# Second SwiGLU product: weight sums and their split as two steps a unit apart, a third raw buffer, operands loaded behind the weights

## Chip, cores, metric

The kernel runs on one core of a Trainium2 chip. The metric is device time in microseconds (us) of one execution.

## What is computed

One inference step of a decoder trunk of two layers, over 1,056 tokens: a prompt of 1,024 and 8 samples of 4. Layer 0 mixes tokens by windowed attention, layer 1 by a gated linear recurrence; behind each mixer stands a SwiGLU of width D_FF = 2,816 on the model width 1,024. All is float32. The part at stake is the second line of this function, `(...) @ w_out`, in both layers:

```python
def swiglu(h, w_in, w_out):
    g, u = jnp.split(h @ w_in, 2, axis=-1)
    return (jax.nn.silu(g) * u) @ w_out
...
xp = xp + swiglu(rms_norm(xp, ffn_norm[layer]), w_ffn_in[layer], w_ffn_out[layer])
xs = xs + swiglu(rms_norm(xs, ffn_norm[layer]), w_ffn_in[layer], w_ffn_out[layer])
```

## The kernel before

Activations lie transposed, model width on the partitions, in three tiles of tokens, 384, 384 and 288 wide. Each float32 product is made of three products of fp32r parts (`mm3`, L291): high by high, high by low, low by high. So every weight is split when it has been loaded into a raw tile: ACT copies it into the high part (L83), VectorE (DVE) subtracts that for the low part (L87). The raw tiles of 128x1024 rotate over two buffers (NRAW); the DMA that fills one (L81) is issued by SyncE (SP).

The second SwiGLU product takes 256 rows of D_FF plainly (`outs`: the operands `h`, read from `hd`), 144 matmuls, and the other 2,560 in five chunks of 512 (`mixed`, `unit`). A unit is a chunk c and a pair of output blocks mp, 20 in a layer. It multiplies 2x2 blocks (two token tiles by two halves of the chunk) in seven products instead of eight, each of 6 matmuls of 384 columns, and the third token tile plainly: two products of 12 matmuls of 288 columns. That makes 66 matmuls; DVE adds each of nine results to the residual stream x (L1001). The last chunk's units have 42, and its plain products come later, between steps of the norm that follows. The seven products use four blocks of the weight itself (`w`) and four sums of its blocks (`ws`). For these `MixSums.prep` runs four GpSimd (POOL) operations on the raw tile in place (L159 to L162), once L87 has read it; then `split` makes a high part on ACT (L329) and a low part on DVE (L330).

A unit's products go to PSUM banks A, B and Dk, eight banks in rotation; A takes three or four of them one after the other, so the next one on A can't begin before DVE's add has read the one ahead. The order of the products in a unit is A (`b11`), Dk (`t3`), B (`b21`), A (`t2`), the first plain one, Dk (`t4`), A (`t1`), the second plain one, A (`b22`).

The other operand of these products, sums of the activations of a chunk, is made earlier and written to DRAM (`od`; the high parts by L870, the low parts by L871). A chunk has nine operands (seven of 768 KB, two of 576 KB), loaded back by `Operand.prep` (L184) into places that are given out and freed: 6 slots of the pool `hp` (`hs`) and 12 of the pool `gp`, 18 in all, two chunks. Weights and sums take one of 6 slots (`wslots`).

TensorE (PE) and SP run in the order of the program (MAN); the order on DVE, ACT and POOL is a scheduler's. Where in the program the loads and splits stand is set by `drive`: it lists what the items need, in order of first use (`needs`, and `ahead` behind them), and behind each item it calls `prep` on the next of the list until one has no place. A unit's `ahead` in chunk c, at mp = 2 and 3, is the next chunk's operands; the first unit's `ahead` is also its own nine operands, and on SP these come in front of the last twelve writes to `od` and of the second weight.

Of the kernel before, what the change touches and what calls it, by code (L numbers as in the profile page):

```python
# [55 lines left out]
class Slots:  # L56
    def __init__(self, names):
        self.free = list(names)
# [8 lines left out]
class Weight:  # L67


    def __init__(self, src, ext=False):  # L70
        self.src, self.ext, self.t, self.slot, self.raw = src, ext, None, None, None

    def prep(self, k, early=False):
        nc = k.nc
        ok = [s for s in k.wslots.free if self.ext or s[0] is k.gw]
        if not ok:
            return False
        self.slot = ok[0]
        k.wslots.free.remove(self.slot)
        raw = self.raw = k.gw.tile([P, 1024], F32, name=k.nm("raw"), tag="raw", bufs=NRAW)  # L80
        nc.sync.dma_start(raw, self.src)  # L81
        self.t = self.slot[0].tile([P, 2, 1024], F32R, name=k.nm("w"), tag=self.slot[1])
        nc.scalar.activation(self.t[:, 0, :], raw, AF.Copy)  # L83
        if early:
            k.early.append((self.t, raw))
        else:
            nc.vector.tensor_tensor(self.t[:, 1, :], raw, self.t[:, 0, :].bitcast(F32), OP.subtract)  # L87
        return True
# [55 lines left out]

class MixSums:
# [5 lines left out]
    def prep(self, k):  # L151
        nc = k.nc
        if not k.wslots.free:
            return False
        self.slot = k.wslots.get()
        r = self.w.raw
        a, b, c, d = (r[:, i * 256:(i + 1) * 256] for i in range(4))
        tt = nc.gpsimd.tensor_tensor
        tt(d, c, d, OP.add)  # L159
        tt(c, a, c, OP.subtract)  # L160
        tt(a, d, a, OP.subtract)  # L161
        tt(b, b, a, OP.subtract)  # L162
        self.t = self.slot[0].tile([P, 2, 1024], F32R, name=k.nm("w"), tag=self.slot[1])
        k.split(self.t[:, 0, :], self.t[:, 1, :], r)
        return True
# [26 lines left out]
class Item:  # L192
    def __init__(self, fn, needs=(), frees=None, ahead=()):
        self.fn, self.needs, self.ahead = fn, list(needs), list(ahead)
# [38 lines left out]
class Kern:  # L233
# [33 lines left out]
    def drive(self, items):  # L267
        need = [w for it in items if isinstance(it, Item) for w in it.needs + it.ahead]
# [4 lines left out]
        for it in items:  # L273
# [4 lines left out]
            else:  # L278
# [5 lines left out]
                while todo and todo[0].prep(self):  # L284
                    todo.pop(0)
# [525 lines left out]
    def ffn_phase(self, l, before, after):  # L811
# [266 lines left out]

        def mixed():
# [5 lines left out]
            for c in range(NCH):  # L1085
                o, last = O[c], c == NCH - 1
                for mp in range(4):
                    w = Weight(I[f"wz{l}"][c, mp], True)
                    s = MixSums(w)
                    end = mp == 3  # L1090
                    nxt = [] if last else {2: O[c + 1][:5], 3: O[c + 1][5:]}.get(mp, [])
                    if last:
                        items.append(Item(lambda a, b, *x, mp=mp: unit(a, b, x, mp, True), [w, s] + o[:7],
                                          [s] + (o[:7] if end else [])))
                        rest.append(Item(lambda a, x, y, mp=mp: [plain(a, (x, y), m, True) for m in (2 * mp, 2 * mp + 1)]
                                         and None, [w] + o[7:], [w] + (o[7:] if end else [])))
                    else:
                        items.append(Item(lambda a, b, *x, mp=mp: unit(a, b, x[:7], mp, False, x[7:]), [w, s] + o,
                                          [w, s] + (o if end else []), nxt))
# [13 lines left out]
        m[0].ahead += m[0].needs[2:]  # L1113
# [380 lines left out]
```

## Time and profile before

| what | value |
|---|---|
| median of 3 runs | 2238.1 us (2237.57 to 2241.82) |
| the profiled execution | 2240.83 us |
| its span in the trace | 2239.0 us |
| mean granted TensorE clock | 0.984 |
| PE, DVE, ACT, POOL busy | 96%, 68%, 45%, 11% of the span |

The span goes from the first to the last instruction that the trace holds; the execution's time has the 1.8 us around it too. Engines are PE (matmul), PEld (weight load, beside PE), DVE, ACT, POOL and SP. In a row of instructions the tiles are written out<-in, with the buffers' numbers left out; a group has its count, busy time and mean ns, and behind the bar the idle time ahead of it and who ended it. The stretch of the second SwiGLU product in chunks is 882 to 1141 us in layer 0 and 1978.4 to 2220.2 us in layer 1.

### The profile page before, as it was taken

How to read it: one execution, taken by the hardware profiler on the slowest of the kernel's cores; microseconds unless marked ns; L12 is line 12 of the kernel's file. 1: busy time of each engine (PE TensorE's matmuls, PEld its weight loads, DVE VectorE, ACT ScalarE, POOL GpSimd, SP SyncE). 2: the span in 40 equal slices, each digit the busy share in tenths (PEclk: the TensorE clock that was granted, in tenths of full speed). 3: DMA queues.
4: the chain of work that ended last, by engine and by line, in shares of the span. 5: the costliest groups of instructions: out<-in, count | busy, mean ns of one | idle time of the engine just before them, and what ended most of it. 6: DMA issues, size and time to landing. Idle time of an engine off the chain costs nothing.

```text
span 2239.0 us, 35153 instructions
## 1 busy us (share of the span) xinstructions
PE 2145.5 (96%) x13608; PEld 2109.3 (94%) x13608; DVE 1514.5 (68%) x2976; ACT 1010.8 (45%) x1835; POOL 242.8 (11%) x328
## 2 busy tenths in 40 slices
PE   9999998999999999989899999999999999999987
PEld 8899988999999999978899989999999999998886
DVE  6877678856566666546685788788666666665556
ACT  5666665434444342111257887744444444411123
POOL 1223230000000001113200000000000000013222
PEclk9999999999999999989999999999999999999998
DMA  5322424133433438445112123431333333575432
GB/s 188 106 96 87 138 76 136 46 125 106 153 129 110 145 128 304 190 156 230 48 49 65 66 67 113 125 93 63 133 133 126 130 136 125 191 270 184 177 130 78
DMA packets 122607, 288.47 MB, mean 129 GB/s; under 512 B 13576, under 2 KB 77640, under 8 KB 122440
## 3 DMA queue, kind: packets, MB, share of 16 engines
q1 hardware_dynamic: 121680, 285.91, 37.1%
q8 instruction: 106, 1.74, 0.3%
q14 instruction: 61, 0.50, 0.1%
q10 hardware_dynamic: 760, 0.33, 0.1%
HBM read 212.34 MB, written 75.84 MB: 129 GB/s over the span
## 4 chain that ended last, share of the span: by engine, by line
PE 75%; DVE 11%; ACT 5%; POOL 5%; issue 2%; DMA 2%; SPq 0%; POOLq 0%; ACTq 0%; DVEq 0%
PE mm L291 71%; DVE w L87 3%; DVE x L1001 2%; ACT w L329 1%; DVE w L330 1%; POOL raw L160 1%; ACT w L83 1%; POOL raw L161 1%; POOL raw L159 1%; POOL raw L162 1%; PE pt L602 1%; PE s L554 1%; DMA raw<-in_wq 1%; DVE s L572 1%; ACT s L579 1%
## 5 line engine op out<-in xcount | busy, mean ns | idle before, releaser
L291 PE MATMUL mm<-xn,w 128*128 128x384 f32 (+1 forms) x5808 | 930.2, 318 | 13.7 <-DVE x L737 4.8
L291 PEld LDWEIGHTS mm<-xn,w 128*128 128x128 f32 x5808 | 904.4, 189 | 19.4 <-issue 5.0
L291 PE MATMUL mm<-o,w 128*128 128x384 f32 (+1 forms) x2640 | 447.4, 330 | 49.8 <-DVE x L1001 35.8
L291 PEld LDWEIGHTS mm<-o,w 128*128 128x128 f32 x2640 | 434.0, 193 | 61.9 <-DVE x L1001 44.5
L87 DVE TENSOR_TENSOR w<-raw,w 128x1024 fp32r<-128x1024 f32 x246 | 299.4, 1223 | 123.6 <-ACT w L83 121.8
L83 ACT ACTIVATE w<-raw 128x1024 fp32r<-128x1024 f32 x248 | 261.5, 1056 | 223.1 <-PE mm L291 128.4
L291 PE MATMUL mm<-T,w 128*128 128x384 f32 x1920 | 351.5, 338 | 0.9 <-ACT sg L969 0.8
L291 PEld LDWEIGHTS mm<-T,w 128*128 128x128 f32 x1920 | 338.8, 188 | 1.6 <-ACT sg L969 1.5
L1001 DVE TENSOR_TENSOR x<-mm,x 128x384 f32<-128x384 f32 (+1 forms) x416 | 211.9, 531 | 119.4 <-PE mm L291 118.4
L159 POOL TENSOR_TENSOR raw<-raw 128x256 f32<-128x256 f32 x40 | 30.6, 764 | 1264.9 <-DVE w L87 810.2
L329 ACT ACTIVATE w<-raw 128x1024 fp32r<-128x1024 f32 x40 | 42.4, 1060 | 259.1 <-POOL raw L162 259.1
L330 DVE TENSOR_TENSOR w<-raw,w 128x1024 fp32r<-128x1024 f32 x40 | 49.9, 1248 | 88.8 <-ACT w L329 88.8
L594 POOL TENSOR_SCALAR s<-s,sm 128x256 f32<-128x256 f32 (+1 forms) x128 | 84.3, 676 | 206.5 <-DVE sm L592 93.5
L291 PE MATMUL mm<-att,w 128*128 128x384 f32 (+1 forms) x576 | 97.3, 324 | 0.3 <-DVE att L330 0.3
L291 PEld LDWEIGHTS mm<-att,w 128*128 128x128 f32 x576 | 91.3, 188 | 2.5 <-DVE att L330 0.5
L291 PE MATMUL mm<-y,w 128*128 128x384 f32 (+1 forms) x576 | 93.5, 322 | 0.0
L291 PEld LDWEIGHTS mm<-y,w 128*128 128x128 f32 x576 | 92.4, 188 | 0.0
L579 ACT ACTIVATE s<-s,sm 128x256 f32<-128x256 f32 (+1 forms) x128 | 61.7, 484 | 47.1 <-DVE sm L576 47.0
L868 ACT ACTIVATE hi<-e 128x384 fp32r<-128x384 f32 x80 | 41.8, 523 | 84.2 <-DVE e L992 28.5
L346 ACT ACTIVATE sq<-x 128x384 f32<-128x384 f32 (+1 forms) x105 | 51.0, 491 | 59.4 <-DVE x L1001 38.8
L116 DVE TENSOR_TENSOR w<-raw,w 128x1024 fp32r<-128x1024 f32 x40 | 48.9, 1223 | 35.5 <-ACT w L114 35.4
L976 ACT ACTIVATE sg<-sg 128x384 f32<-128x384 f32 x40 | 21.0, 525 | 91.4 <-DVE sg L975 91.4
(210 smaller groups left out, 2381.7 us busy)
## 6 DMA issues: line engine op xcount, KB each, us to landing
o<-od SPq DMA_DIRECT2D x70, 768.0 KB, 8.5
od<-hi SPq DMA_DIRECT2D x140, 192.0 KB, 2.0
raw<-in_wg SPq DMA_DIRECT2D x44, 512.0 KB, 4.0
raw<-in_wu SPq DMA_DIRECT2D x44, 512.0 KB, 5.0
raw<-in_wz SPq DMA_DIRECT2D x40, 512.0 KB, 4.2
od<-e SPq DMA_DIRECT2D x80, 192.0 KB, 2.0
raw<-in_wq SPq DMA_DIRECT2D x24, 512.0 KB, 3.6
raw<-in_wo SPq DMA_DIRECT2D x24, 512.0 KB, 3.5
```

What stands on the lines that cost most here:

```text
L83: nc.scalar.activation(self.t[:, 0, :], raw, AF.Copy)
L87: nc.vector.tensor_tensor(self.t[:, 1, :], raw, self.t[:, 0, :].bitcast(F32), OP.subtract)
L116: tt(d[:, 1, :], g, d[:, 0, :].bitcast(F32), OP.subtract)
L159: tt(d, c, d, OP.add)
L291: mm = lambda *a, **k: self.nc.tensor.matmul(*a, skip_group_check=more, **k)
L329: nc.scalar.activation(hi, src, AF.Copy)
L330: nc.vector.tensor_tensor(lo, src, hi.bitcast(F32), OP.subtract)
L346: nc.scalar.activation(sq[:, :W], self.xview(t, kb), AF.Square)
L579: nc.scalar.activation(s[:, j, :N], s[:, j, :N], AF.Exp, bias=sm[:, 1, j:j + 1], accum_out=sm[:, 3, j:j + 1])
L594: nc.gpsimd.tensor_scalar(s[:, j, :N], s[:, j, :N], sm[:, 4, j:j + 1], 1.0, op0=OP.mult, op1=OP.mult)
L868: nc.scalar.activation(hi.bitcast(F32R), src, AF.Copy)
L1001: tt(x, ps[:, :WID[t]], x, OP.add)
```

## The change

- The four POOL steps become a step of their own (`Mix`), and `MixSums` only splits.
- Each item has a list `order` in place of `ahead`. Unit u's is: its weight and sums, the next unit's weight and sums, three of the next chunk's operands (from mp = 1 on), then the split of its own sums, then its operands. So the split of sums u comes behind the load, the split and the sums of weight u+1. 
- Every third weight has its raw tile not in the two rotating buffers but in a slot of `hp`, which it takes from the operands' places for good (`third`): 17 are left.
- `drive` no longer stops at an operand that has no place, but goes on to what stands behind it in the list. It still stops at a weight or sums without a place.
- The first chunk's operands are no longer ahead; they come behind the first two weights and the first split of sums.

Lines move by 1 in front of the change and by up to 18 behind it: L81 becomes L82, L83 L84, L87 L88, L184 L195, L329 and L330 L347 and L348, L870 and L871 L888 and L889, L1001 L1019; POOL's four are L156 to L159.

```diff
--- before.py
+++ after.py
@@ -67,17 +67,18 @@
 class Weight:
 
 
-    def __init__(self, src, ext=False):
-        self.src, self.ext, self.t, self.slot, self.raw = src, ext, None, None, None
+    def __init__(self, src, ext=False, place=None):
+        self.src, self.ext, self.place, self.t, self.slot, self.raw = src, ext, place, None, None, None
 
     def prep(self, k, early=False):
         nc = k.nc
         ok = [s for s in k.wslots.free if self.ext or s[0] is k.gw]
-        if not ok:
+        raw = ok and (self.place() if self.place else k.gw.tile([P, 1024], F32, name=k.nm("raw"), tag="raw", bufs=NRAW))
+        if not raw:
             return False
+        self.raw = raw
         self.slot = ok[0]
         k.wslots.free.remove(self.slot)
-        raw = self.raw = k.gw.tile([P, 1024], F32, name=k.nm("raw"), tag="raw", bufs=NRAW)
         nc.sync.dma_start(raw, self.src)
         self.t = self.slot[0].tile([P, 2, 1024], F32R, name=k.nm("w"), tag=self.slot[1])
         nc.scalar.activation(self.t[:, 0, :], raw, AF.Copy)
@@ -142,26 +143,36 @@
         self.slots.put(self.slot)
 
 
-class MixSums:
+class Mix:
 
 
     def __init__(self, w):
-        self.w, self.t, self.slot = w, None, None
+        self.w, self.t = w, None
 
     def prep(self, k):
-        nc = k.nc
-        if not k.wslots.free:
-            return False
-        self.slot = k.wslots.get()
         r = self.w.raw
         a, b, c, d = (r[:, i * 256:(i + 1) * 256] for i in range(4))
-        tt = nc.gpsimd.tensor_tensor
+        tt = k.nc.gpsimd.tensor_tensor
         tt(d, c, d, OP.add)
         tt(c, a, c, OP.subtract)
         tt(a, d, a, OP.subtract)
         tt(b, b, a, OP.subtract)
+        self.t = r
+        return True
+
+
+class MixSums:
+
+
+    def __init__(self, w):
+        self.w, self.t, self.slot = w, None, None
+
+    def prep(self, k):
+        if not k.wslots.free:
+            return False
+        self.slot = k.wslots.get()
         self.t = self.slot[0].tile([P, 2, 1024], F32R, name=k.nm("w"), tag=self.slot[1])
-        k.split(self.t[:, 0, :], self.t[:, 1, :], r)
+        k.split(self.t[:, 0, :], self.t[:, 1, :], self.w.raw)
         return True
 
     def free(self, k):
@@ -190,8 +201,9 @@
 
 
 class Item:
-    def __init__(self, fn, needs=(), frees=None, ahead=()):
-        self.fn, self.needs, self.ahead = fn, list(needs), list(ahead)
+    def __init__(self, fn, needs=(), frees=None, order=None):
+        self.fn, self.needs = fn, list(needs)
+        self.order = self.needs if order is None else list(order)
         self.frees = self.needs if frees is None else list(frees)
         self.halves = [self]
 
@@ -265,7 +277,7 @@
                 self.nc.gpsimd.tensor_tensor(w[:, 1, c], raw[:, c], w[:, 0, c].bitcast(F32), OP.subtract)
 
     def drive(self, items):
-        need = [w for it in items if isinstance(it, Item) for w in it.needs + it.ahead]
+        need = [w for it in items if isinstance(it, Item) for w in it.order]
         todo = self.todo = []
         for w in need:
             if w not in todo:
@@ -281,8 +293,14 @@
                 post = it.fn(*[w.t for w in it.needs])
                 for w in it.frees:
                     w.free(self)
-                while todo and todo[0].prep(self):
-                    todo.pop(0)
+                i = 0
+                while i < len(todo):
+                    if todo[i].prep(self):
+                        todo.pop(i)
+                    elif isinstance(todo[i], Operand):
+                        i += 1
+                    else:
+                        break
                 if post:
                     post()
 
@@ -1076,27 +1094,37 @@
             return [Item(lambda a, b, h, t=t: h_out(a, b, h, t), w + [h[t]],
                          (w if t == 2 else []) + [h[t]]) for t in range(NT)]
 
+        def third():
+
+            if "raw" not in T:
+                if not hs.free:
+                    return None
+                T["raw"] = hs.free.pop()
+            t = self.hp.tile([P, 4 * WMAX], F32, name=self.nm("raw"), tag=T["raw"])
+            return t[:, :1024]
+
         def mixed():
 
             pools = [(lambda: self.hp, hs), (lambda: self.gp, self.slots)]
             O = [[Operand(lambda c=c, i=i: OD[c, i], WMAX, pools) for i in KEEP] + [Operand(lambda c=c, i=i: OD[c, i], WID[2], pools) for i in range(2)]
                  for c in range(NCH)]
             items, rest = [], []
-            for c in range(NCH):
-                o, last = O[c], c == NCH - 1
-                for mp in range(4):
-                    w = Weight(I[f"wz{l}"][c, mp], True)
-                    s = MixSums(w)
-                    end = mp == 3
-                    nxt = [] if last else {2: O[c + 1][:5], 3: O[c + 1][5:]}.get(mp, [])
-                    if last:
-                        items.append(Item(lambda a, b, *x, mp=mp: unit(a, b, x, mp, True), [w, s] + o[:7],
-                                          [s] + (o[:7] if end else [])))
-                        rest.append(Item(lambda a, x, y, mp=mp: [plain(a, (x, y), m, True) for m in (2 * mp, 2 * mp + 1)]
-                                         and None, [w] + o[7:], [w] + (o[7:] if end else [])))
-                    else:
-                        items.append(Item(lambda a, b, *x, mp=mp: unit(a, b, x[:7], mp, False, x[7:]), [w, s] + o,
-                                          [w, s] + (o if end else []), nxt))
+            units = [(c, mp) for c in range(NCH) for mp in range(4)]
+            w = [Weight(I[f"wz{l}"][c, mp], True, third if (4 * c + mp) % 3 == 2 else None) for c, mp in units]
+            x = [Mix(y) for y in w]
+            s = [MixSums(y) for y in w]
+            for u, (c, mp) in enumerate(units):
+                o, last, end = O[c], c == NCH - 1, mp == 3
+                order = [w[u], x[u]] + ([w[u + 1], x[u + 1]] if u + 1 < len(units) else [])
+                order += (O[c + 1][3 * mp - 3:3 * mp] if mp and not last else []) + [s[u]] + o
+                if last:
+                    items.append(Item(lambda a, b, *y, mp=mp: unit(a, b, y, mp, True), [w[u], s[u]] + o[:7],
+                                      [s[u]] + (o[:7] if end else []), order))
+                    rest.append(Item(lambda a, y, z, mp=mp: [plain(a, (y, z), m, True) for m in (2 * mp, 2 * mp + 1)]
+                                     and None, [w[u]] + o[7:], [w[u]] + (o[7:] if end else [])))
+                else:
+                    items.append(Item(lambda a, b, *y, mp=mp: unit(a, b, y[:7], mp, False, y[7:]), [w[u], s[u]] + o,
+                                      [w[u], s[u]] + (o if end else []), order))
             return items, rest
 
         n0, n1 = after
@@ -1110,7 +1138,6 @@
             L += blocks(f)
         p = outs()
         m, q = mixed()
-        m[0].ahead += m[0].needs[2:]
         L += p
         for i, x in enumerate(m):
             if l == 0 and i < DB:
```


The order on PE and on POOL stays as it was. Three places elsewhere:

DVE in layer 1, start of the eighth unit, before. L87 makes the low part of the weight two units on, L330 that of its sums (both from raw_20759), and L1001 adds a bank (mm) to a tile of x:

```order
L87 TENSOR_TENSOR w_20761<-raw_20759,w_20761 128x1024
L1001 TENSOR_TENSOR x_1987<-mm_20771,x_1987 128x384
L1001 TENSOR_TENSOR x_3467<-mm_20773,x_3467 128x384
L1001 TENSOR_TENSOR x_1987<-mm_20772,x_1987 128x384
L330 TENSOR_TENSOR w_20768<-raw_20759,w_20768 128x1024
L1001 TENSOR_TENSOR x_1987<-mm_20771,x_1987 128x384
L1001 TENSOR_TENSOR x_4440<-mm_20802,x_4440 128x288
```

The same unit now; its nine adds are the rows L1019. L348 in the first row makes the low part of the next unit's sums, L88 that of the weight three units on, and L348 in the last row that of the sums two units on:

```order
L348 TENSOR_TENSOR w_20763<-raw_20578,w_20763 128x1024
L88 TENSOR_TENSOR w_20768<-raw_20766,w_20768 128x1024
L1019 TENSOR_TENSOR x_1987<-mm_20775,x_1987 128x384
L1019 TENSOR_TENSOR x_3467<-mm_20777,x_3467 128x384
L1019 TENSOR_TENSOR x_1987<-mm_20776,x_1987 128x384
L1019 TENSOR_TENSOR x_1987<-mm_20775,x_1987 128x384
L1019 TENSOR_TENSOR x_4440<-mm_20806,x_4440 128x288
L1019 TENSOR_TENSOR x_1987<-mm_20777,x_1987 128x384
L1019 TENSOR_TENSOR x_3467<-mm_20775,x_3467 128x384
L1019 TENSOR_TENSOR x_4440<-mm_20834,x_4440 128x288
L1019 TENSOR_TENSOR x_3467<-mm_20775,x_3467 128x384
L348 TENSOR_TENSOR w_20863<-raw_20674,w_20863 128x1024
```

Three adds stood between a weight's low part and its sums'. Now the unit's nine adds follow one another without a split between them, and the sums' split at its end reads raw_20674, whose weight was split before the unit.

DVE in layer 0, the fifth unit, before. L330 makes the low part of that unit's sums, L87 that of the next unit's weight:

```order
L1001 TENSOR_TENSOR x_1986<-mm_9994,x_1986 128x384
L330 TENSOR_TENSOR w_9791<-raw_9782,w_9791 128x1024
L1001 TENSOR_TENSOR x_3466<-mm_9996,x_3466 128x384
L1001 TENSOR_TENSOR x_1986<-mm_9995,x_1986 128x384
L1001 TENSOR_TENSOR x_1986<-mm_9994,x_1986 128x384
L87 TENSOR_TENSOR w_9878<-raw_9876,w_9878 128x1024
L1001 TENSOR_TENSOR x_4439<-mm_10025,x_4439 128x288
```

and now. The first L88 and L348, both from raw_9789, make the low parts of the next unit's weight and sums, the second L88 that of the weight after it:

```order
L1019 TENSOR_TENSOR x_1986<-mm_10002,x_1986 128x384
L1019 TENSOR_TENSOR x_3466<-mm_10004,x_3466 128x384
L88 TENSOR_TENSOR w_9791<-raw_9789,w_9791 128x1024
L1019 TENSOR_TENSOR x_1986<-mm_10003,x_1986 128x384
L1019 TENSOR_TENSOR x_1986<-mm_10002,x_1986 128x384
L348 TENSOR_TENSOR w_9982<-raw_9789,w_9982 128x1024
L88 TENSOR_TENSOR w_9885<-raw_9883,w_9885 128x1024
L1019 TENSOR_TENSOR x_4439<-mm_10033,x_4439 128x288
```

A unit's sums are now split in the unit ahead of it, and their low part stands two adds behind the weight's.

SP in layer 1, ahead of the first unit, before: the last three of the first chunk's nine operands (L184), then the first two of twelve writes to od (L870 for a high part, L871 for a low one). The first weight (in_wz) stands ahead of the nine, the second behind the twelve:

```order
L184 DMA o_19772<-od_15246 128x1536
L184 DMA o_19774<-od_15247 128x4x288
L184 DMA o_19776<-od_15248 128x4x288
L870 DMA od_15277<-hi_19787 128x384
L871 DMA od_15277<-e_2583_19640 128x384
```

and now: the last four of the twelve writes, then the first operands of the nine. The first two weights stand ahead of the twelve:

```order
L888 DMA od_15281<-hi_19795 128x384
L889 DMA od_15281<-e_2563_19453 128x384
L888 DMA od_15282<-hi_19800 128x384
L889 DMA od_15282<-t_19771 128x384
L195 DMA o_19858<-od_15240 128x1536
L195 DMA o_19860<-od_15241 128x1536
L195 DMA o_19862<-od_15242 128x1536
L195 DMA o_19864<-od_15243 128x1536
```

The nine operands have moved behind the twelve writes, the second weight in front of them.

More of the change, by code (lines that the diff above doesn't have):

```diff
@@ L142, in free @@
         self.slots.put(self.slot)
+class Mix:
+    def __init__(self, w):
+        self.w, self.t = w, None
+    def prep(self, k):
+        r = self.w.raw
+        a, b, c, d = (r[:, i * 256:(i + 1) * 256] for i in range(4))
+        tt = k.nc.gpsimd.tensor_tensor
+        tt(d, c, d, OP.add)
+        tt(c, a, c, OP.subtract)
+        tt(a, d, a, OP.subtract)
+        tt(b, b, a, OP.subtract)
+        self.t = r
+        return True
 class MixSums:
@@ L155, in prep @@
         self.slot = k.wslots.get()
-        r = self.w.raw
-        a, b, c, d = (r[:, i * 256:(i + 1) * 256] for i in range(4))
-        tt = nc.gpsimd.tensor_tensor
[L159 to L162, printed above, removed]
         self.t = self.slot[0].tile([P, 2, 1024], F32R, name=k.nm("w"), tag=self.slot[1])
-        k.split(self.t[:, 0, :], self.t[:, 1, :], r)
+        k.split(self.t[:, 0, :], self.t[:, 1, :], self.w.raw)
         return True
```

## Prediction

> **What bounds the kernel now.** I read the page's head first, then the stretches of the second SwiGLU product (layer 0, layer 1) and the waits of PE inside them, then one unit on the timeline. The columns of a stretch are length, busy us (instructions) of PE, PEld, DVE, ACT and POOL, granted clock, DMA share, GB/s.
>
> ```profile
> span 2239.0 us, 35153 instructions
> PE 2145.5 (96%) x13608; PEld 2109.3 (94%) x13608; DVE 1514.5 (68%) x2976; ACT 1010.8 (45%) x1835; POOL 242.8 (11%) x328
> ...
> 882.00:1141.00 259.00, 228.48 (x1341) 221.02 (x1339) 151.97 (x255) 53.51 (x65) 61.03 (x78) 0.95 0.43 160
> 1978.40:2220.20 241.80, 221.77 (x1340) 216.68 (x1339) 148.62 (x252) 56.89 (x71) 62.18 (x79) 0.98 0.43 160
> 905.00:929.00 24.00, 24.00 (x154) 24.00 (x153) 12.98 (x24) 2.01 (x2) 2.95 (x4) 1.00 0.16 59
> 2000.00:2018.00 18.00, 18.00 (x114) 18.00 (x113) 11.56 (x18) 3.07 (x3) 6.03 (x7) 1.00 0.21 74
> ```
>
> PE is busy 96% of the span, so only its gaps and its slower clock can be won. The same product takes 259.0 us in layer 0 and 241.8 us in layer 1 for the same number of matmuls, and stretches without a gap run at 24.00/154 = 0.156 and 18.00/114 = 0.158 us a matmul (0.157 below). A unit of 66 matmuls would take 10.36 us. The waits of PE (total us, times, longest) are, in layer 0 and then in layer 1:
>
> ```profile
> PE mm L291 <- DVE x L1001: 15.9, 12, 3.5
> PE mm L291 <- ACT w L329: 10.0, 3, 3.3
> PE mm L291 <- DVE w L87: 3.1, 3, 1.4
> PE mm L291 <- DVE w L330: 0.8, 3, 0.3
> ```
>
> ```profile
> PE mm L291 <- DVE x L1001: 19.9, 16, 3.6
> ```
>
> That is 15.9 + 10.0 + 3.1 + 0.8 = 29.8 us and 19.9 us. The clock adds to it. The next rows are the slow stretches, four of layer 0 and three of layer 1:
>
> ```profile
> 893.00:905.00 12.00, 9.79 (x50) 9.79 (x51) 6.96 (x13) 2.12 (x2) 2.17 (x2) 0.86 1.03 414
> 929.00:941.00 12.00, 8.13 (x29) 6.99 (x28) 4.58 (x7) 2.00 (x2) 2.91 (x4) 0.72 0.35 120
> 971.00:1005.00 34.00, 24.93 (x122) 22.96 (x123) 13.65 (x21) 4.01 (x4) 8.57 (x12) 0.80 0.32 115
> 1094.00:1104.00 10.00, 7.39 (x35) 7.08 (x34) 5.46 (x9) 3.99 (x6) 0.89 (x2) 0.83 0.17 52
> 1989.00:1999.00 10.00, 7.33 (x34) 7.33 (x35) 6.57 (x11) 2.12 (x2) 2.55 (x3) 0.83 1.01 372
> 2018.00:2028.00 10.00, 6.84 (x34) 6.52 (x33) 5.55 (x8) 2.11 (x2) 4.48 (x6) 0.83 0.55 208
> 2173.00:2186.00 13.00, 10.39 (x51) 10.02 (x50) 8.11 (x15) 5.12 (x8) 3.93 (x6) 0.87 0.01 1
> ```
>
> Busy time less matmuls x 0.157 is the loss: 1.9, 3.6, 5.8 and 1.9 in layer 0, 2.0, 1.5 and 2.4 in layer 1. The fourth and the last lie in the fifth chunk, where I estimate a matmul at 0.175, which leaves 1.3 and 1.5. So 12.6 and 5.0 us. In all 29.8 + 19.9 + 12.6 + 5.0 = 67.3 us can go; nothing else in the two stretches is slack.
>
> **Why PE waits.** One unit of layer 1 on the timeline (start, length, engine, instruction, idle before it and who ended it):
>
> ```profile
> 2061.87 10.82 PE L291 MATMUL mm<-o,w 128*128 128x384 f32 x66 [1.05 <-DVE x L1001]
> ...
> 2066.35 1.22 DVE L87 TENSOR_TENSOR w<-raw,w 128x1024 fp32r<-128x1024 f32 x1
> ...
> 2067.65 0.75 POOL L159 TENSOR_TENSOR raw<-raw 128x256 f32<-128x256 f32 x1 [8.65 <-DVE w L87]
> ...
> 2070.88 1.06 ACT L329 ACTIVATE w<-raw 128x1024 fp32r<-128x1024 f32 x1 [5.00 <-POOL raw L162]
> 2071.97 1.23 DVE L330 TENSOR_TENSOR w<-raw,w 128x1024 fp32r<-128x1024 f32 x1 [2.37 <-ACT w L329]
> 2073.11 1.38 DVE L1001 TENSOR_TENSOR x<-mm,x 128x384 f32<-128x384 f32 x3
> ...
> 2073.72 0.97 PE L291 MATMUL mm<-o,w 128*128 128x384 f32 x4 [1.03 <-DVE x L1001]
> ```
>
> L330, the low part of the sums, stands three adds behind its weight's L87 on DVE, but the chain L87, four POOL steps, ACT L329 takes 2071.97 - 2066.35 = 5.6 us. DVE stands 2.37 us with the unit's adds queued behind. By columns (384 and 288) the 10.36 us of a unit make 1.04 us for a product of 6 matmuls and 1.55 for a plain one of 12. Four of the unit's products share bank A; of the adds on A the one behind the split here is the second (`t2`), and PE's third (`t1`) needs the bank 1.55 + 1.04 = 2.6 us after `t2`'s end. PE stopped at 2073.72 - 1.03 = 2072.69, so `t2` had ended at 2070.1; the add came at 2073.11, 3.0 us late, and PE saw 1.03 of it. An add on A may thus be 2.0 us late for nothing in this place, by the same working 2 x 1.04 less the add itself (1.38 us for three above, some 0.5 each) = about 1.5 in the first place (`b11`) and 1.0 in the third. In all, DVE waits for L329 in the two stretches (busy, mean ns | idle before):
>
> ```profile
> L330 DVE TENSOR_TENSOR w<-raw,w 128x1024 fp32r<-128x1024 f32 x19 | 23.7, 1249 | 42.2 <-ACT w L329 42.2
> L330 DVE TENSOR_TENSOR w<-raw,w 128x1024 fp32r<-128x1024 f32 x19 | 23.7, 1249 | 41.0 <-ACT w L329 41.0
> ```
>
> **The change part by part.** *Sums and split a unit apart, third raw buffer.* Nothing is added on DVE, ACT or POOL: the same 40 splits and 160 sums, so their busy time is 0 either way. In layer 1 the sums' low part now stands a whole unit ahead of its use and a unit behind its weight, so POOL and ACT are done when DVE gets there and the 41 us of standing go. DVE then has 1.22 + 1.23 = 2.45 us of splits a unit in front of adds. Next late is such a pair put together: the first add behind it is up to 2.45 us late, 2.45 - 1.5 = 0.95 of which PE sees; I take 0.8 for each of five such places, 4 us, and 1.6 and 0.8 for two places with a further split or a weight behind operand loads: about 6.5 us left in layer 1. In layer 0 close pairs stay: in unit 4 the sums' low part stands two adds behind its weight's, one fewer than above, so DVE stands about 2.37 + 1 = 3.4 us and then has two splits, 2.45, ahead of the unit's fifth add; of these 5.9 us I give PE 2.9 (half: the fifth add's bank isn't needed at once), and 1.9 us of clock with it (as in 893 to 905). With the smaller waits of units 1, 8 and 9 and the tail I take 8.1 + 1.9 = 10 us.
>
> *Operands behind the weights.* The first chunk's nine loads used to be issued ahead of the od writes. SP, PE and the landing of those nine in layer 1 now:
>
> ```profile
> 1947.67 7.52 SPq L184 DMA_DIRECT2D o<-od  x9
> 1956.11 5.78 SPq L870 DMA_DIRECT2D od<-hi  x1
> ...
> 1976.84 0.42 SPq L81 DMA_DIRECT2D raw<-in_wz  x1
> ...
> 1955.50 23.15 PE L291 MATMUL mm<-h,w 128*128 128x384 f32 x144
> 1978.48 9.60 PE L291 MATMUL mm<-o,w 128*128 128x384 f32 x60
> ...
> DMA to landing us min/median/max: 6.5/10.5/14.9
> ```
>
> They land from 1947.67 + 6.5 = 1954.2 to 1954.27 + 14.9 = 1969.2, a step of about 1.9 us. Now they stand behind 12 od writes, the last of which waits for a DVE step that I put at 1964 (from the splits and four adds ahead of it, by the lengths above). So they land from about 1970 to 1984, under the 144 matmuls (1955.5 to 1978.65) and the first products. The sixth load is needed by the second product at 1979.4, the ninth at about 1983. By that step the wait is 0 to 2.6 us a layer; a transfer rate free of other loads speaks for the lower end, and I take 1. If the cover were gone it would be the whole lateness, some 5 us. In return the second weight leaves SP right behind the first, ahead of the od writes, rather than at 1976.84, and the two longest waits, which stood behind it in the first unit, go:
>
> ```profile
> 895.21 34.78 PE L291 MATMUL mm<-o,w 128*128 128x384 f32 x206 [3.48 <-DVE x L1001]
> ...
> 1991.67 27.09 PE L291 MATMUL mm<-o,w 128*128 128x384 f32 x156 [3.58 <-DVE x L1001]
> ```
>
> *Seventeen operand places for eighteen.* The ninth operand and the next three stand on SP until a unit ends, and one weight a chunk stands behind them:
>
> ```profile
> L81 SPq DMA_DIRECT2D raw<-in_wz x1: 689/689/689, 2125.7 to 2125.7; - x1
> ...
> DMA to landing us min/median/max: 9.3/9.3/9.3
> ...
> L160 POOL TENSOR_TENSOR raw<-raw x40: 724/738/1810, 859.0 to 2185.7; 128x256 f32<-128x256 f32 x40
> ```
>
> The first two rows are a weight issued at 2125.7, behind operand loads, that landed 9.3 us later. The new order puts the low part of such a weight on DVE ahead of the eighth add of the chunk's first unit, some 54 x 0.157 = 8.5 us into it, and the adds behind it wait. Landing at 9.3 and split by ACT at 10.4, it makes the add 1.9 us late; less the 1.0 to 1.5 that cost nothing that is some 0.6, and I took 0.8 above. Landed like most weights, behind nothing, it costs 0.
>
> The POOL row shows one step of 1.81 us against a median of 0.738. The Trainium skill ("SBUF — State Buffer", section "Who interferes with whom") says that a VectorE operation with two SBUF inputs and a GpSimd operation that reads SBUF shut one another out for a whole instruction; the trace agrees so far as a POOL step of 738 ns reaches 1810. By that rule alone every POOL step that now meets a split could take 1.07 us longer, still under a unit's distance.
>
> I set 2 us aside for stretched POOL steps. **Sum:** left are 6.5 + 10 + 2 x 1 + 2 = 20.5, so 67.3 - 20.5 = 46.8 go. The profiled execution took 2240.83 us; 2240.83 - 46.8 = 2194. It lies 2.7 us above the median of 2238.1, so the median comes to about 2191, and I say 2192.
>
> **The rivals.** *The waits only move* (0.20): close pairs of splits decide wherever the scheduler leaves them, and two splits together cost most of 0.95 wherever they meet. Then 40 x 0.75 = 30 us stay, with the 10 of layer 0, 2 at the starts and 2 of POOL, 44 us: 23 saved, 2215. For it: in layer 0 the pairs of units 1, 4 and 8 are still close. Against it: DVE is busy only 148.62 of 241.80 us.
>
> *The clock does not come back* (0.06): if only gaps as long as 3.5 us cost clock, just the two stretches behind 3.48 and 3.58 us return (1.9 + 2.0 of 17.6), and 13.7 less is saved: about 2205. The clocks behind shorter gaps speak against it:
>
> ```profile
> 934.58 1.01 PE L291 MATMUL mm<-o,w 128*128 128x384 f32 x2 [3.34 <-ACT w L329]
> ...
> 2178.70 14.43 PE L291 MATMUL mm<-o,w 128*128 128x384 f32 x72 [2.60 <-DVE x L1001]
> ```
>
> Behind 2.60 us the granted clock is 0.87, behind 3.34 us 0.72. The Trainium skill ("TensorE: Matmul & The Clock Gate", section "Part 1: The HAM clock gate (the "warmup" mystery)") has the clock halved after at least one idle window of about 3.4 us; by that rule it would be this rival, and the trace does not bear it out, with 0.87 after 2.60 us.
>
> *Slower* (0.07): the weight behind the blocked operand loads comes too late. The ninth load and three more wait for the unit's end on SP; if the weight lands 3 us later than the 9.3 us above, the add behind it is 1.9 + 3 us late, of which PE sees 4.9 - 1.3 = 3.6 and loses 1.9 of clock: 5.5, four times a layer, 44 in all. With 3.5 a layer at the starts (2.6 and the reserve of one) it is 51 against 46.8 saved: 2242. It decides from a landing some 12 us behind the unit's start.
>
> *It doesn't do what it says* (0.05): the scheduler puts the sums' low part back behind its weight, as in layer 0's unit 4, in most units; 2238.
>
> **How the numbers follow.** My forecast has 0.62, with 2178 to 2201 its own range: from a third of the 20.5 left (2238.1 - 67.3 + 7) to 30 left (3.2 more at the starts, and twice the five places at 1.0: 6 more). The range reaches on to the second case, 2178 to 2218, and leaves out its upper end, the slower case and no effect. A measurement of this kernel tells about 0.2%, 4.5 us, from no change. Faster by more: 0.62 + 0.20 + 0.06 = 0.88; same 0.05; slower 0.07.
>
> **What would show it.** In the profile after: DVE's idle time ahead of the sums' low part falls from 41 and 42 us to a few in layer 1 and about 10 in layer 0; PE's waits fall from 29.8 and 19.9 to about 9 and 7; the stretches shorten from 259 and 242 to about 230 and 226 with a granted clock near 1.00. It is wrong if PE waits more than 2 us for the first chunk's operands, if the adds wait for a weight that lands over 12 us into a unit, or if PE waits for the adds as often as now.

## The result, and the profile after

The changed kernel takes 2186.74 us (median of 4 runs, 2186.04 to 2188.04) against 2239.19 (4 runs, one more than in the table before, 2237.57 to 2241.82): ratio 0.9765, 95% interval 0.9748 to 0.9782, some 52 us. The profiled execution took 2187.09 us, 53.7 less than the one before.

The head of the page, and the two stretches of the second SwiGLU product, layer 0 first, with the way between them (columns as in the prediction):

```profile
span 2185.0 us, 35145 instructions
PE 2128.5 (97%) x13608; PEld 2097.2 (96%) x13608; DVE 1514.5 (69%) x2976; ACT 1008.8 (46%) x1835; POOL 244.5 (11%) x328
```

```profile
879.00:1102.80 223.80, 216.44 (x1340) 212.17 (x1338) 147.74 (x249) 50.82 (x61) 55.10 (x74) 1.00 0.51 190
1102.80:1943.50 840.70, 828.10 (x5142) 824.40 (x5143) 596.20 (x1150) 464.09 (x767) 13.32 (x14) 0.99 0.34 111
1943.50:2166.10 222.60, 217.11 (x1340) 213.71 (x1338) 147.62 (x251) 54.93 (x70) 59.92 (x75) 0.99 0.48 182
```

With the same bounds (first and last matmul of the product) the stretches before were 258.3 and 241.8 us, the way between them 838.0:

```profile
882.10:1140.40 258.30, 228.38 (x1340) 220.92 (x1338) 151.37 (x253) 52.94 (x63) 61.03 (x78) 0.95 0.43 160
1140.40:1978.40 838.00, 827.22 (x5142) 824.40 (x5143) 593.30 (x1146) 462.48 (x764) 8.66 (x10) 0.99 0.34 113
```

So 258.3 - 223.8 = 34.5 us went from layer 0 and 241.8 - 222.6 = 19.2 from layer 1, together 53.7, the whole gain. Outside the stretches two differences cancel: the first stretch begins 3.1 us earlier, and the way between is 2.7 us longer. It begins anywhere from 878.8 to 882.2 us in the twelve profiles of this document, so 3 us there mean nothing. DVE's busy time is the same 1514.5 us as before; what went is waiting. PE's waits in layer 0, then in layer 1:

```profile
PE mm L309 <- DVE x L1019: 5.3, 9, 2.4
PE mm L309 <- DMA o<-od: 1.9, 3, 0.9
```

```profile
PE mm L309 <- DVE x L1019: 3.2, 8, 1.4
PE mm L309 <- DMA o<-od: 2.1, 1, 2.1
```

DVE's group of the sums' low part, in the same order (busy, mean | idle before):

```profile
L348 DVE TENSOR_TENSOR w<-raw,w 128x1024 fp32r<-128x1024 f32 x19 | 23.2, 1221 | 13.3 <-ACT w L347 13.2
L348 DVE TENSOR_TENSOR w<-raw,w 128x1024 fp32r<-128x1024 f32 x19 | 23.6, 1243 | 3.2 <-ACT w L347 3.1
```

PE waits 7.2 and 5.3 us instead of 29.8 and 19.9; DVE stands 13.3 and 3.2 us instead of 42.2 and 41.0. What is left holds a kind of wait that was not there before: 1.9 and 2.1 us for operands at the two starts.

### The profile page after: what moved, and what is told of

Read it like the earlier page. It is cut to its first block, busy times and chain, and to the rows that moved or that the text cites. A ratio compares the mean times of both kernels' runs of the same rounds, so it can differ in the third digit from the quotient of the medians.

```text
span 2185.0 us, 35145 instructions
## 1 busy us (share of the span) xinstructions
PE 2128.5 (97%) x13608; PEld 2097.2 (96%) x13608; DVE 1514.5 (69%) x2976; ACT 1008.8 (46%) x1835; POOL 244.5 (11%) x328
## 4 chain that ended last, share of the span: by engine, by line
PE 76%; DVE 12%; ACT 5%; DMA 3%; issue 2%; POOL 2%; SPq 0%; ACTq 0%; POOLq 0%; DVEq 0%
PE mm L309 73%; DVE w L88 2%; DMA o<-od 1%; ACT w L84 1%; DVE x L1019 1%; DVE w L348 1%; DVE xs L414 1%; PE pt L620 1%; PE s L572 1%; ACT s L597 1%; DVE s L590 1%; DVE xn L348 1%; DMA raw<-in_wu 1%; ACT w L347 0%; DVE acc L365 0%
## 5 line engine op out<-in xcount | busy, mean ns | idle before, releaser
L309 PE MATMUL mm<-xn,w 128*128 128x384 f32 (+1 forms) x5808 | 929.7, 318 | 13.3 <-DVE x L755 4.6
L309 PE MATMUL mm<-o,w 128*128 128x384 f32 (+1 forms) x2640 | 430.9, 323 | 12.8 <-DVE x L1019 8.5
L309 PEld LDWEIGHTS mm<-o,w 128*128 128x128 f32 x2640 | 422.3, 188 | 20.0 <-DVE x L1019 14.8
L88 DVE TENSOR_TENSOR w<-raw,w 128x1024 fp32r<-128x1024 f32 x246 | 299.9, 1225 | 120.3 <-ACT w L84 119.3
L84 ACT ACTIVATE w<-raw 128x1024 fp32r<-128x1024 f32 x248 | 261.2, 1056 | 191.3 <-PE mm L309 75.0
L1019 DVE TENSOR_TENSOR x<-mm,x 128x384 f32<-128x384 f32 (+1 forms) x416 | 213.3, 530 | 135.6 <-PE mm L309 134.7
L156 POOL TENSOR_TENSOR raw<-raw 128x256 f32<-128x256 f32 x40 | 30.9, 771 | 1195.7 <-DVE w L88 733.3
L347 ACT ACTIVATE w<-raw 128x1024 fp32r<-128x1024 f32 x40 | 42.5, 1062 | 260.7 <-PE mm L309 133.9
L886 ACT ACTIVATE hi<-e 128x384 fp32r<-128x384 f32 x80 | 41.8, 522 | 62.7 <-DVE e L1010 29.6
L348 DVE TENSOR_TENSOR w<-raw,w 128x1024 fp32r<-128x1024 f32 x40 | 49.8, 1244 | 19.9 <-ACT w L347 19.8
L887 DVE TENSOR_TENSOR t<-t,hi 128x384 fp32r<-128x384 f32 x60 | 34.7, 578 | 40.8 <-ACT hi L886 39.6
```

The source lines that it names most:

```text
L309: mm = lambda *a, **k: self.nc.tensor.matmul(*a, skip_group_check=more, **k)
L347: nc.scalar.activation(hi, src, AF.Copy)
L348: nc.vector.tensor_tensor(lo, src, hi.bitcast(F32), OP.subtract)
L886: nc.scalar.activation(hi.bitcast(F32R), src, AF.Copy)
L887: tt(src.bitcast(F32R), src, hi, OP.subtract)
L1019: tt(x, ps[:, :WID[t]], x, OP.add)
```

## The experiments

Each kernel ran beside the kernel before on the same chip; the ratio is to that. Stretches are those of the profiled execution, between the same matmuls as above. The changed kernel's own were 223.8, then 840.7 between them, and 222.6.

**1. The split of the sums right behind the sums.**

```diff
-order = [w[u], x[u]] + ([w[u + 1], x[u + 1]] if u + 1 < len(units) else [])
-order += (O[c + 1][3 * mp - 3:3 * mp] if mp and not last else []) + [s[u]] + o
+order = [w[u], x[u], s[u]] + ([w[u + 1], x[u + 1]] if u + 1 < len(units) else [])
+order += (O[c + 1][3 * mp - 3:3 * mp] if mp and not last else []) + o
```

> The changed kernel with the split of the sums put right behind the sums in the list, ahead of the next weight, third buffer and order of the loads otherwise kept. Theory (DVE standing for the sums' high part, with adds behind it, is what cost PE its 1 us a unit): DVE's idle time ahead of the sums' low part is back at 30 to 45 us a layer, PE waits about 1 us in two units of three, 2207 to 2222. Rival (the gain is from the third buffer and the earlier loads): 2192 or less, with DVE standing and PE not waiting.

Measured: 2227.43 us (4 runs), ratio 0.9943 (0.9929 to 0.9956). DVE's group of the sums' low part and PE's waits, in layer 1:

```profile
L348 DVE TENSOR_TENSOR w<-raw,w 128x1024 fp32r<-128x1024 f32 x18 | 22.1, 1225 | 39.5 <-ACT w L347 39.5
```

```profile
PE mm L309 <- DVE x L1019: 17.9, 17, 2.6
PE mm L309 <- DMA o<-od: 1.3, 3, 0.5
```

DVE stands 39.5 us again (41.0 before the change), and PE waits 17.9 us in 17 waits, with layer 1 at 239.1 us against 241.8 before the change. In layer 0, whose stretch is 247.4 us, DVE stands 41.8 us, and PE waits:

```profile
PE mm L309 <- DVE x L1019: 20.2, 13, 4.5
```

The time lies above my range of 2207 to 2222; in layer 0 the waits reach 4.5 us. The theory stands, and the rival (DVE standing and PE not waiting) is out: third buffer and load order, kept here, recover 2.7 us of layer 1's 19.2 and 10.9 of layer 0's 34.5. By the medians the place of the split in the list is worth 40.7 us of the 52.

**2. Sums and split in one step, the order kept.** `Mix` does nothing, and `MixSums` makes the four POOL steps and the split.

```diff
 class Mix:
...
-        tt(d, c, d, OP.add)
-        tt(c, a, c, OP.subtract)
-        tt(a, d, a, OP.subtract)
-        tt(b, b, a, OP.subtract)
...
 class MixSums:
...
+        tt(d, c, d, OP.add)
+        tt(c, a, c, OP.subtract)
+        tt(a, d, a, OP.subtract)
+        tt(b, b, a, OP.subtract)
```

> The changed kernel with the four POOL steps made where the split is made, in one step as before the change, the list of loads and splits left as it is. The order on DVE is the same but for one place in layer 0. Theory (it is the place of the split in the list that counts, and POOL takes up the sums as soon as its own order and the weight's low part allow): 2185 to 2189, no difference. Rival (the sums' own step is what starts POOL early): POOL starts later, DVE stands for the sums again, 2200 or more.

Measured: 2186.46 us (4 runs), ratio 0.9762 (0.9748 to 0.9775): no difference. That the sums are a step of their own is worth nothing by itself; what counts is where the split stands in the list, behind the next weight.

**3. Without the third raw buffer.**

```diff
-w = [Weight(I[f"wz{l}"][c, mp], True, third if (4 * c + mp) % 3 == 2 else None) for c, mp in units]
+w = [Weight(I[f"wz{l}"][c, mp], True, None) for c, mp in units]
```

> The changed kernel without the third raw buffer: every weight's raw tile is in the two rotating buffers, and all 18 operand places are there. Theory (the gain comes from the order of the splits on DVE alone; in layer 1 the low part of the sums still stands a unit away from its weight's): layer 1 within 3 us of the changed kernel, layer 0, where four sums stand close behind their weights, up to 6 slower: 2186 to 2194. Rival (the third buffer is what lets a weight be loaded early enough): weights land late, DVE stands for them, and the time comes back to 2205 or more.

Measured: 2203.43 us (5 runs), ratio 0.9835 (0.9822 to 0.9848), 17 us more. The theory's range, 2186 to 2194, missed it, and it is near the rival's number, 2205 or more. But nearly all of it is in layer 0 (the profiled execution is the slowest of the five, 6.4 us above the median):

```profile
881.70:1123.80 242.10, 223.83 (x1340) 217.65 (x1338) 149.72 (x253) 50.80 (x61) 57.02 (x74) 0.96 0.48 176
1965.40:2188.90 223.50, 215.13 (x1340) 212.53 (x1338) 148.50 (x250) 55.93 (x70) 58.46 (x75) 1.00 0.49 182
```

Layer 0 is 18.3 us longer than in the changed kernel; layer 1 is within 1 us, so two buffers are enough there. In layer 0, one weight from its load (SP's row, with its landing) to the matmul that waits, on the timeline:

```profile
L82 SPq DMA_DIRECT2D raw<-in_wz x1: 338/338/338, 947.7 to 947.7; - x1
...
DMA to landing us min/median/max: 4.0/4.0/4.0
```

```profile
960.60 1.04 ACT L84 ACTIVATE w<-raw 128x1024 fp32r<-128x1024 f32 x1
...
970.73 1.22 DVE L88 TENSOR_TENSOR w<-raw,w 128x1024 fp32r<-128x1024 f32 x1
...
972.02 0.74 POOL L156 TENSOR_TENSOR raw<-raw 128x256 f32<-128x256 f32 x1 [12.43 <-DVE w L88]
975.21 1.06 ACT L347 ACTIVATE w<-raw 128x1024 fp32r<-128x1024 f32 x1 [13.57 <-POOL raw L159]
...
976.32 1.01 PE L309 MATMUL mm<-o,w 128*128 128x384 f32 x2 [3.35 <-ACT w L347]
```

The weight landed at 947.7 + 4.0 = 951.7, and its high part was made by 961.6; its low part came at 970.73, 9 us later, since it stands there in DVE's order, behind ten adds. The rival's reason (a load that comes late) is not what the rows show. What differs in layer 0 is that eight pairs of copies of the caches stand on SP between the weights (L784 and L785). This led to the next two.

**4. The same with the copies behind the units; 5. the kernel before with that move alone.** Both have this edit:

```diff
-            if l == 0 and i < DB:
-                L.append(lambda b=i: self.caches(b))
             L.append(x)
...
         if l == 0:
             L += [lambda m=m: self.square(2, m) for m in range(KB)]
+            L += [lambda b=b: self.caches(b) for b in range(DB)]
```

> The kernel without the third raw buffer, and the eight pairs of cache copies that layer 0 puts on SP between its first eight units now behind the last of them. Nothing else differs, but the splits of layer 0 now stand on DVE as those of layer 1. Theory (the third buffer counts in layer 0 alone, since only there the copies on SP between the weights make the scheduler place the splits late): the stretch of layer 0 falls from 242 to about 224 us, as in layer 1, and the time to 2183 to 2189. Rival (two buffers are short in layer 0 because the copies' own traffic holds up the weights, or for another reason of that layer): 2197 or more, with the stretch of layer 0 above 235.

> The kernel before, with layer 0's cache copies behind its units and nothing else. Theory (the 17 us by which layer 0 was slower than layer 1 came from the copies' place, through the order on DVE): the stretch of layer 0 falls from 258 to about 242 us, and the time to 2219 to 2227. Rival (layer 0 is slower for other reasons): 2233 or more.

Measured: for 4, 2188.81 us (4 runs), ratio 0.9766 (0.9753 to 0.978); for 5, 2229.87 us (5 runs), ratio 0.9946 (0.9933 to 0.9958). The stretches of layer 0 and the way to layer 1, of the first kernel and then of the second:

```profile
880.30:1099.90 219.60, 215.09 (x1340) 212.53 (x1338) 149.77 (x253) 52.08 (x61) 57.39 (x74) 1.00 0.52 190
1099.90:1946.50 846.60, 829.65 (x5142) 825.45 (x5143) 596.15 (x1147) 464.12 (x767) 13.37 (x14) 0.99 0.34 112
```

```profile
879.10:1120.40 241.30, 220.94 (x1340) 215.12 (x1338) 150.86 (x253) 54.07 (x63) 60.66 (x78) 0.99 0.47 171
1120.40:1965.50 845.10, 829.89 (x5142) 825.67 (x5143) 593.13 (x1146) 462.44 (x764) 8.65 (x10) 0.99 0.34 112
```

Without the third buffer layer 0 falls from 242.1 to 219.6 us, and in the kernel before from 258.3 to 241.3, as long as layer 1. So the 17 us by which layer 0 was the slower one came from the copies' place. DVE's group of the sums' low part in layer 0, in experiment 3 and then in 4:

```profile
L348 DVE TENSOR_TENSOR w<-raw,w 128x1024 fp32r<-128x1024 f32 x19 | 23.9, 1257 | 21.9 <-ACT w L347 21.9
L348 DVE TENSOR_TENSOR w<-raw,w 128x1024 fp32r<-128x1024 f32 x19 | 24.4, 1282 | 2.9 <-ACT w L347 2.8
```

That the copies act through the order on DVE, not by their traffic, two things in the traces show. In both kernels the splits and adds of layer 0's twenty units now follow one another on DVE exactly as layer 1's do; with the copies between the units they don't. And the weights of layer 0 had landed as soon with the copies between them: after 4.0 us (median, at most 13.5) in experiment 3, after 3.6 (at most 13.4) in experiment 4. Why the scheduler places the splits otherwise, no run shows. Both kernels give 6 to 7 us back on the way to layer 1 (846.6 us against 840.7, 845.1 against 838.0), so the second one missed its range. In both, 2.9 us of that are PE's waits for layer 1's first weights, as under 8.

**6. The first chunk's operands ahead of the first split of sums.**

```diff
-order += (O[c + 1][3 * mp - 3:3 * mp] if mp and not last else []) + [s[u]] + o
+order += (o if u == 0 else []) + (O[c + 1][3 * mp - 3:3 * mp] if mp and not last else []) + [s[u]] + o
```

> The changed kernel with one edit: the first chunk's nine operands stand right behind the first two weights, ahead of the first split of sums and so ahead of the last twelve writes to od. Theory (the change gives back part of its gain at the two starts, because those loads now leave SP behind the writes): PE's waits for operands, 1.9 and 2.1 us in the changed kernel, go, with the 1.7 us of half clock behind the second, 5.7 in all; the low part of the sums of the sixth unit in layer 0 also moves away from its weight's, up to 2.5 more. About 2180, 2178 to 2182. Rival (the waits are the price of loading the second weight early, whatever the order behind it): the operands arrive in time but the writes to od, now behind nine loads, hold up the high parts on ACT and PE waits elsewhere: 2186 or more.

Measured: 2184.11 us (4 runs), ratio 0.9747 (0.9733 to 0.976). PE's waits, layer 0 and layer 1:

```profile
PE mm L309 <- DVE x L1019: 4.7, 11, 1.1
```

```profile
PE mm L309 <- DVE x L1019: 3.8, 9, 1.1
```

The waits for operands are gone, and the stretches are 220.9 and 219.2 us, 2.9 and 3.4 less; but the medians differ by 2.6 us, not by 5.7, so the time lies above its range of 2178 to 2182, and the intervals of the two ratios overlap. In this profile the first stretch began at 881.1 us instead of 879.0 and the way between was 842.1 instead of 840.7; the rival's waits do not show there, since ahead of either stretch PE has none. So the term is shown by the waits; its size, 3 to 6 us, is not fixed.

**7. The next chunk's operands listed as before the change.**

```diff
-order += (O[c + 1][3 * mp - 3:3 * mp] if mp and not last else []) + [s[u]] + o
+order += [s[u]] + o + ([] if last else {2: O[c + 1][:5], 3: O[c + 1][5:]}.get(mp, []))
```

> The changed kernel with the next chunk's operands listed as before the change: five behind a chunk's third unit's own needs, four behind its fourth's, instead of three at a time ahead of the split of the sums. Theory (the order of the splits carries the gain, not the spreading of the loads): 2184 to 2190. Rival (spread loads are what lets the weights land in time): weights land behind five loads, DVE stands for them with adds behind it at each of four chunk changes, 2195 or more.

Measured: 2193.15 us (5 runs), ratio 0.9793 (0.9779 to 0.9807). Neither range holds it. It is 6.4 us above the changed kernel by the medians, but in the profile the two stretches are only 2.0 us longer each (225.8 and 224.6), and 3.1 us lie ahead of the first one, where this edit changes nothing. So I take 4 to 6 us for how the loads are listed. The timeline of layer 0 shows the longest wait:

```profile
934.21 1.22 DVE L348 TENSOR_TENSOR w<-raw,w 128x1024 fp32r<-128x1024 f32 x1 [3.41 <-ACT w L347]
935.35 1.22 DVE L88 TENSOR_TENSOR w<-raw,w 128x1024 fp32r<-128x1024 f32 x1
...
936.86 1.60 DVE L88 TENSOR_TENSOR w<-raw,w 128x1024 fp32r<-128x1024 f32 x1
939.44 2.93 PE L309 MATMUL mm<-o,w 128*128 128x384 f32 x8 [3.94 <-DVE x L1019]
```

Other loads put another weight next, so three splits meet in the fifth unit, and PE waits 3.94 us, not 2.45, with a granted clock of 0.98 over the stretch against 1.00. The rival's reason isn't it: DVE stands for a weight's high part not at all in layer 0 and 0.6 us in layer 1, where weights landed after 10.2 us at most, against 14.4 in the changed kernel.

**8. Both moves; 9. the copies in the first product; 10. the changed kernel again.** Experiment 8 has the move of 4 and the edit of 6, with the third buffer. Experiment 9 has the edit of 6 too, but the copies stand behind eight blocks of layer 0's first SwiGLU product:

```diff
         for f in range(NPL, NF):
             L += blocks(f)
+            if l == 0 and 2 <= f - NPL < 2 + DB:
+                L.append(lambda i=f - NPL - 2: self.caches(i))
...
-            if l == 0 and i < DB:
-                L.append(lambda b=i: self.caches(b))
```

> The changed kernel with both moves: the first chunk's operands ahead of the first split of sums, and layer 0's cache copies behind its units. Theory: layer 0's stretch comes down to layer 1's, 219 us from 220.8, so 2180 to 2184. Rival (the copies behind the units hold up layer 1's first weights on SP): PE waits at the start of layer 1, 2186 or more.

> The first chunk's operands ahead of the first split of sums, and layer 0's eight pairs of cache copies moved into the first SwiGLU product of layer 0, one pair behind each of eight blocks, instead of behind the units. Theory (behind the units they delayed layer 1's first weights by 4 to 5 us, here SP has time for them): both stretches at about 219 us and the way from the one to the other at 841 to 842 us, so 2179 to 2183. Rival (a copy on SP between weights makes the scheduler place splits late wherever it stands, so the first product of layer 0 loses what the second gains): 2185 or more.

> The changed kernel again, for a comparison on the same chip: 2185 to 2189.

Measured, in this order: 2185.34 us (5 runs), ratio 0.9752 (0.9739 to 0.9765); 2180.48 us (4 runs), ratio 0.9739 (0.9726 to 0.9752); and 2185.79 us (4 runs), ratio 0.9754 (0.974 to 0.9767). PE's waits for layer 1's first weights in experiment 8, and then the stretches of experiment 9:

```profile
PE mm L309 <- ACT w L84: 2.3, 1, 2.3
...
PE mm L309 <- DVE w L88: 0.6, 1, 0.6
```

```profile
880.40:1099.50 219.10, 215.38 (x1340) 212.27 (x1339) 149.52 (x250) 51.62 (x61) 59.47 (x74) 1.00 0.48 178
1099.50:1940.80 841.30, 828.63 (x5143) 825.10 (x5143) 595.29 (x1150) 464.36 (x767) 12.97 (x14) 0.99 0.34 113
1940.80:2159.90 219.10, 215.38 (x1340) 212.27 (x1338) 148.44 (x251) 55.27 (x70) 60.65 (x75) 1.00 0.47 177
```

Behind the units the copies cost PE 2.9 us for layer 1's first weights. The time of 8 lies between its two ranges and within the scatter of the changed kernel's; the reason that its rival gave is the one that the rows show. In the first product they cost nothing that shows, and both layers run at 219.1 us. Experiment 9 is the fastest of all: 2180.48 us, 5 to 6 below the two medians of the changed kernel, and each of its runs is below each of theirs, though the intervals of the ratios overlap a little.

No run tests alone the part of the change by which `drive` goes on past an operand that has no place.

## Why the prediction was right, point by point

- **What can go.** The ceiling of 67.3 us held. Left are PE's waits of 7.2 and 5.3 us and 1.7 of clock, 14.2, where I had 20.5; 67.3 - 14.2 = 53.1, and the profiled executions differ by 53.7. The total is partly luck: of the terms left, layer 1's pairs (3.2 for 6.5), layer 0 (5.3 for 10) and POOL (0 for 2) came in 10.0 us smaller, the starts (5.7 for 2) 3.7 larger.
- **DVE standing with adds behind it.** Right, and shown by experiment 1: with the split put back, layer 1 has 39.5 us of standing and 17 waits of 1 us on average again.
- **Pairs of splits.** Five at 0.8 and one each at 1.6 and 0.8 in layer 1: seven waits came in at 0.2 to 0.4 and one at 1.4, 3.2 in all against 6.5. The one is a sums' split and two weights' in a row, on the timeline of the changed kernel:

```profile
1980.12 1.22 DVE L348 TENSOR_TENSOR w<-raw,w 128x1024 fp32r<-128x1024 f32 x1
1981.25 2.35 DVE L88 TENSOR_TENSOR w<-raw,w 128x1024 fp32r<-128x1024 f32 x2
1982.55 1.64 POOL L156 TENSOR_TENSOR raw<-raw 128x256 f32<-128x256 f32 x1 [4.34 <-DVE w L88]
...
1984.13 0.45 PE L309 MATMUL mm<-o,w 128*128 128x384 f32 x1 [1.37 <-DVE x L1019]
```

  Here L348 has no idle time ahead of it: its high part was ready. I had taken 1.6 for this place. That the others cost less than 0.8 each I put down to splits that begin before the product they hold up has ended; no run tells this apart.
- **Layer 0.** The two adds between weight and sums in the fifth unit:

```profile
932.67 1.22 DVE L348 TENSOR_TENSOR w<-raw,w 128x1024 fp32r<-128x1024 f32 x1 [3.41 <-ACT w L347]
933.81 1.22 DVE L88 TENSOR_TENSOR w<-raw,w 128x1024 fp32r<-128x1024 f32 x1
...
936.38 4.48 PE L309 MATMUL mm<-o,w 128*128 128x384 f32 x24 [2.45 <-DVE x L1019]
```

  DVE stands 3.4 us and PE 2.45, as worked out (3.4 and 2.9). The clock did not drop behind it in this profile. In experiments 2 and 10 it did, behind the same wait. I had 10 us and the layer has 5.3.
- **What had no term: the third buffer.** "Nothing is added" held for busy time (DVE 1514.5 us in both), but the sum does not say what the buffer brings. Without it the time is 17 us longer, nearly all of it in layer 0 (experiment 3). I explained layer 0's extra 17 us by its longer waits and its clock and did not ask why they were in that layer alone; they go when the cache copies are moved (4 and 5), and the changed kernel still has the copies in the old place. With the copies there, the third buffer takes 18.3 us off layer 0's stretch; with the copies moved, the layer does as well without it (219.6 us). The total came out because the order of the changed kernel, which I read, already held that effect.
- **The starts.** I took 1 us each within 0 to 2.6. Measured: 1.9, and 2.1 with 1.7 of clock behind it; in the repeat (experiment 10) 0.6 and 1.6. The waits lie within the bounds, but I gave no clock to them. One of my own signs of being wrong, more than 2 us of waiting for these operands, came up in layer 1 by 0.1 us: the cover was thinner than I had it. Experiment 6 shows that the waits can be had away.
- **Stretched POOL steps and the late weight.** PE's list has no wait for a split of the sums, so the POOL step of 1.64 us above and the 2 us that I set aside for such steps cost nothing that shows. The weights of layer 1 from its third on, in the changed kernel:

```profile
DMA to landing us min/median/max: 3.4/7.6/14.4
```

  One, issued at 2036.6 among a chunk's operand loads, landed 14.4 us after its issue, more than the 9.3 + 3 that I gave the slower case. DVE stood 0.8 us in all for weights in that layer, and PE's list has no wait for a weight: the price that I put on such a landing is not borne out.
- **The rivals.** The waits did not just move (12.5 us are left of 49.7), and the clock came back: 1.00 and 0.99 in the two stretches, from 0.95 and 0.98. What the clock depends on is below.

## What to carry to other kernels

A step that an in-order engine waits for costs what is queued behind it, not what it does: put a dependent pair a full round apart on that engine, and read the distance from its order rather than from the steps' names. Where two copies of the same code take different times, first look for what else stands on the queues there. Here eight pairs of DMAs between the weights went with another order of the splits on DVE, 17 us to the worse before the change and 22 without the third buffer.

## What the runs showed of the hardware

The clock changes on a grid. In all twelve traces every change of the granted clock past the start lies on a grid of 3.413 us (within 0.03), at another place in the program in each, and they go with how busy PE was in the window ahead. In the changed kernel, two waits and the windows behind them:

```profile
934.59:938.00 3.41, 1.62 (x9) 1.62 (x10) 2.37 (x6) 0.00 (x0) 2.65 (x4) 1.00 1.01 408
938.00:941.42 3.42, 3.13 (x18) 2.81 (x17) 2.31 (x4) 2.01 (x2) 0.28 (x1) 1.00 1.02 408
1944.95:1948.36 3.41, 1.51 (x9) 1.54 (x10) 1.41 (x3) 0.00 (x0) 0.00 (x0) 1.00 1.03 389
1948.36:1951.78 3.42, 3.42 (x13) 3.42 (x12) 0.98 (x3) 0.00 (x0) 0.00 (x0) 0.50 1.07 408
```

and the first of the two waits in experiment 2, where it lies otherwise on the grid:

```profile
932.94:936.36 3.42, 1.14 (x9) 0.91 (x7) 3.42 (x5) 0.80 (x1) 1.01 (x2) 1.00 1.03 429
936.36:939.77 3.41, 3.23 (x10) 3.23 (x11) 1.28 (x4) 1.32 (x2) 1.90 (x3) 0.50 1.01 407
```

A wait of 2.45 us that a grid line divides leaves PE busy for 1.62 us of a window and costs nothing; the same wait within one window leaves 1.14, and the next window has half clock, some 1.7 us lost. A shorter wait of 2.12 us (1.51 busy) cost the same. I divided all twelve traces by their grids from 800 us on, and took the windows at full clock in which PE was idle for over 28%: up to 40% idle, 1 of 61 was followed by half clock; above 40 and up to 55%, 10 of 38; above that, 53 of 53. The waits of 1.03 us (30%) never cost clock. The Trainium skill ("TensorE: Matmul & The Clock Gate", section "Part 1: The HAM clock gate (the "warmup" mystery)") has a window of 3,413 ns that runs freely; the traces agree on the window and its length, and show that a window need not be idle throughout: over 55% idle was enough each time. So a kernel's waits have a price that depends on where they fall, and two executions of one kernel can differ by 1.7 us for it.
